# Feed-forward output products summed straight into the four quarters of the result, their operand differences by VectorE, and the recurrence's gate products grouped at its last chunk

## Chip, cores and metric

One core of a Trainium2 chip runs the whole kernel in one launch. The metric is the device time of that launch in microseconds, the median of the runs.

## What is computed

Two transformer blocks on one sequence of 1024 tokens and 1024 channels, all in float32. Each ends in a feed-forward part and only that and the second block's gated recurrence matter here:

```python
m = rmsnorm(h, g)
hid = square(relu(m @ w_in))       # 1024 -> 4096
h = h + hid @ w_out                # 4096 -> 1024, then the next norm

z = rms_norm(x, ln1_g) @ w_in + b_in               # second block
q, k, v, u, y_branch, g_att, g_rec = split(z)      # u, y, gates: 1024 channels each
u = centred_depthwise_conv(u, conv_w, conv_b)      # 4 taps
h_f, h_b = rg_lru(u, ..., reverse=False), rg_lru(u, ..., reverse=True)   # scans over tokens
y_rec = ((h_f + h_b) * gelu(y_branch)) @ w_rec_o
y_att = neighbourhood_attention(q, k, v, rpb) @ w_att_o
mixed = sigmoid(g_att) * y_att + sigmoid(g_rec) * y_rec
```

## The kernel before

Channels lie on partitions, tokens on the free axis: an activation of 1024 x 1024 is 8 tiles of 128 x 1024. Each float32 operand is split into a high and a low part, the high by ScalarE (`whi`, `obh`), the low by VectorE from it (`wlo`, `obl`, both line 478 for these blocks), and a product is three matmuls per 128 of its depth, high x high, high x low, low x high. The order of instructions on each engine is the program's own: `run` goes through a list of jobs, one product each, and before a job issues the weight splits that later jobs need (`ahead`, 3 jobs for the output products) and weight loads, all on SP's queue. 36 tiles of 128 x 1024 rotate for everything else (`z`).

**Feed-forward output.** The depth of 4096 goes in four blocks b = 0 to 3 (`N_BLK` is 3, the last one), each of 1024. In a block the 2 x 2 product of quarters is made of seven products of quarters (numbers 1, 2, 3, 6, 7, 5, 4, `SEVEN_OUT`) of sums and differences of the operands; each product is done for the four column pairs p of the result, 28 steps a block. A step is 12 matmuls of 512 columns into one of four PSUM banks (`seven`, line 1122); then deferred work (`todo`); at p = 0 and 2 the operand of the next product is prepared (`out_prep`: ScalarE and VectorE split it, and after four of the seven products GpSimd subtracts one quarter of the activation from another, lines 1200 to 1206, 128 x 1024 each); then the result is taken out of PSUM. In blocks 0 to 2 (`out_step`) that is one sum per step into one of seven partial sums `xs` (line 1274, VectorE; in block 0 ScalarE copies instead for products 1, 6, 7 and 5, line 1272). In block 2 the seven sums are mixed into the four quarters, by six GpSimd sums and two VectorE sums per p (line 1241). The residual `res` comes from HBM into `xs` before it is used (line 1238), in halves, mainly in block 0. The last block (`block_step` with `last_ev`) sums straight into the four quarters c11, c12, c21, c22 of `h`: eight VectorE sums, three GpSimd sums (lines 1327 to 1331) and one ScalarE copy per p. In the second feed-forward part the last block has an order of its own (`end_block`): product 2's operands are made beside product 1, its products are done late.

**The recurrence.** Channels go in 8 chunks c: a product for u, one for y, then gate products (`gate_job`), which only store their scaled result. 16 gate products are made: 6 before the chunks, 10 among them, one per chunk and two in chunks 3 and 7. Beside the products runs background work, generators in three lanes; `tick` after each six matmuls gives `rate` credits, and a whole credit takes one step of each lane. `lru_front` of a chunk (16 steps: convolution, the polynomial of gelu by GpSimd at lines 1741 and 1742, the gate matrices on TensorE at line 1766, their sigmoids by ScalarE at line 1753 behind the one of line 1759) starts when the chunk's y is there; `lru_back` (13 steps: ScalarE's functions, VectorE's scans, a store of the result at line 1801) follows it. The rate is 0.65, in chunk 7 1.0. `att2_split` prepares the attention's output operands during the last gate product. Then come eight attention output products (`att_o_job`, rate 1.1; `mixed` is written at line 1853 of it), which also load the recurrence's results, and the recurrence's output products.

Of the kernel before, what the change touches and what calls it, by code (L numbers as in the profile page):

```python
# [31 lines left out]
RATE_L = (0.65, 1.0)  # L32
# [164 lines left out]
class Kern:  # L197
# [992 lines left out]
    def out_prep(self, b, i, kk):  # L1190

        G = self.nc.gpsimd
        hi, lo = self.ob[b, i, kk] = self.u("obh"), self.u("obl")

        def q(e, a):
            return self.hraw[b, kk, e, a]

        self.hilo(q(0, 0) if i in (1, 7) else q(0, 1) if i == 5 else q(1, 0) if i in (2, 4) else q(1, 1), hi, lo)
        if i == 1:
            G.tensor_tensor(q(0, 1), q(0, 1), q(0, 0), ALU.subtract)  # L1200
        elif i == 3:
            G.tensor_tensor(q(1, 1), q(1, 1), q(0, 1), ALU.subtract)
        elif i == 6:
            G.tensor_tensor(q(0, 0), q(1, 1), q(0, 0), ALU.subtract)
        elif i == 7:
            G.tensor_tensor(q(1, 0), q(1, 0), q(1, 1), ALU.subtract)
            del self.hraw[b, kk, 0, 0], self.hraw[b, kk, 1, 1]
        elif i == 5:
            del self.hraw[b, kk, 0, 1]
        elif i == 4:  # L1210
            del self.hraw[b, kk, 1, 0]
# [6 lines left out]
    def out_step(self, un, b, p):  # L1218


        nc = self.nc
        V, G = nc.vector, nc.gpsimd
        i = un.i
        j = SEVEN_OUT.index(i)
        sl = slice((p % 2) * H, (p % 2) * H + H)

        def operand(k):
            ks = slice((k % 2) * H, (k % 2) * H + H)
            return tuple(x[:, ks] for x in self.ob[b, i, k // 2])

        def x(q):
            return self.xs[q, p // 2][:, sl]

        def alloc(q, e=None, a=None):
            if p % 2 == 0:
                self.xs[q, p // 2] = self.z(nm="xs")
            if e is not None:
                nc.sync.dma_start(x(q), half(self.res[2 * p + e], a))

        def add(eng, d, q):  # L1240
            eng.tensor_tensor(x(d), x(d), x(q), ALU.add)  # L1241

        def mix():
            if i == 2:
                add(G, 2, 1)
            elif i == 6:
                add(G, 6, 1)
                self.todo.append(lambda: self.todo.append(lambda: add(V, 3, 6)))
            elif i == 7:
                add(G, 7, 6)  # L1250
                alloc(0, 1, 1)
            elif i == 5:
                add(G, 3, 5)
                add(G, 5, 7)
            elif i == 4:
                add(G, 4, 7)
                add(V, 5, 0)
                self.h[2 * p], self.h[2 * p + 1] = [x(2), x(3)], [x(4), x(5)]

        def fn():  # L1260
            ps = self.seven(un, operand)
            todo, self.todo = self.todo, []
            for f in todo:
                f()
            for kk in AHEAD[p]:
                self.out_prep(*((b, SEVEN_OUT[j + 1]) if j < 6 else (b + 1, 1)), kk)
            self.next_loads(b + 1, i, p)
            if b == 0 and i in (1, 2, 5):
                alloc(*{1: (2, 0, 0), 2: (3, 0, 1), 5: (4, 1, 0)}[i])
            if b == 0 and i not in (2, 3, 4):  # L1270
                alloc(i)
                nc.scalar.activation(x(i), ps, AF.Copy)
            else:
                V.tensor_tensor(x(i), ps, x(i), ALU.add)  # L1274
            if b == N_BLK - 1:
                mix()
        return fn

    def block_step(self, un, b, p, ev, after, prep=True):
# [6 lines left out]
        def fn():  # L1286
            ps = self.seven(un, operand)
# [3 lines left out]
            if prep and i != SEVEN_OUT[-1]:  # L1291
                self.prep_step(b, i, p)()
            elif after:
                after(p)
# [16 lines left out]
    def last_ev(self, after):  # L1311
# [4 lines left out]
        def ev(i, p, ps):  # L1316
            u = self.half_u(i, p)
            (c11, c12), (c21, c22) = self.h[2 * p], self.h[2 * p + 1]
# [18 lines left out]
            after(i, p)  # L1337
        return ev

    def ff(self, pr, w1, w2, gname, after):  # L1340
# [44 lines left out]
        ev = self.last_ev(after)  # L1385
        n = 28
        for i in SEVEN_OUT:
            for p in range(4):
                un = two[i, p // 2]
                pr.job([un] if p % 2 == 0 else [], self.block_step(Pick(un, p % 2), N_BLK, p, ev, None),  # L1390
# [3 lines left out]
    def end_block(self, pr, two):  # L1394
# [3 lines left out]
        ev = self.last_ev(self.end_after)  # L1398
# [3 lines left out]
        for n, (i, p) in enumerate(order):  # L1402
# [5 lines left out]
            if i == 2:  # L1408
                pr.job(uns, self.prep_step(N_BLK, i, p), ahead)
                later.append(self.block_step(w, N_BLK, p, ev, None, False))  # L1410
# [4 lines left out]
            fn = self.end_step(w, p, (0, H // 2)) if i == 4 else self.block_step(w, N_BLK, p, ev, None)  # L1415
# [388 lines left out]
    def gate_job(self, un, dst, m, last=False):  # L1804
# [3 lines left out]
        def fn():  # L1808
            if last:
                self.bg[2].append(self.att2_split())  # L1810
# [3 lines left out]
            if last:  # L1814
# [66 lines left out]
    def program(self):  # L1881
        pr = Prog()
        self.h = [None] * NC
        self.hraw, self.ob, self.xs, self.todo = {}, {}, {}, []
# [136 lines left out]
        for c in range(NC):  # L2021
            pr.rate = RATE_L[c > NC - 2]
# [3 lines left out]
            gate_jobs(2 if c in (3, 7) else 1)  # L2026
# [223 lines left out]
```

## Time and profile before

| | |
|---|---|
| median of the runs | 2988.58 us (2981.69 to 2990.8, 3 runs) |
| the profiled execution | 2983.65 us, of which its span from the first to the last instruction 2981.9 us |
| busy share of the span | TensorE 96%, VectorE 64%, ScalarE 39%, GpSimd 37% |
| granted TensorE clock, mean | 0.985 |
| moved between HBM and the core | 402.35 MB |

First feed-forward output: 1074.5 to 1392 us of the span, blocks of about 76 us; second: 2637 to 2966. The recurrence's chunks: about 1736 to 2083, then the attention output products to 2136. PE is TensorE's matmuls, DVE VectorE, ACT ScalarE, POOL GpSimd, SP the engine that issues the DMAs. A row of a wait names who waited and who released it; a time in brackets in a row in order of time is how long the engine stood idle before it, and after the arrow who ended that. The share of the clock is that of TensorE's full speed.

### The profile page before, as it was taken

How to read it: one execution, taken by the hardware profiler on the slowest of the kernel's cores; microseconds unless marked ns; L12 is line 12 of the kernel's file. 1: busy time of each engine (PE TensorE's matmuls, PEld its weight loads, DVE VectorE, ACT ScalarE, POOL GpSimd, SP SyncE). 2: the span in 40 equal slices, each digit the busy share in tenths (PEclk: the TensorE clock that was granted, in tenths of full speed). 3: DMA queues.
4: the chain of work that ended last, by engine and by line, in shares of the span. 5: the costliest groups of instructions: out<-in, count | busy, mean ns of one | idle time of the engine just before them, and what ended most of it. 6: DMA issues, size and time to landing. Idle time of an engine off the chain costs nothing. (4 is left out here: it accounts for less than half of the span.)

```text
span 2981.9 us, 35224 instructions
## 1 busy us (share of the span) xinstructions
PE 2874.7 (96%) x13422; PEld 2357.2 (79%) x13422; DVE 1916.4 (64%) x2325; ACT 1170.6 (39%) x1786; POOL 1116.5 (37%) x554
## 2 busy tenths in 40 slices
PE   9999999999899999998999999998899899999987
PEld 8888787888788888876777788886788788888866
DVE  6434554666865577799743337878555855577797
ACT  3322234223354454335133325555423344444334
POOL 0020112644444443486300005455144444443486
PEclk9999999999999999999999999999999999999998
DMA  4221136776233254442423221221686233254442
GB/s 161 75 75 47 66 120 224 252 283 248 85 113 107 105 203 164 149 155 78 133 78 98 85 78 61 71 78 51 250 307 221 85 113 114 99 209 166 148 155 85
DMA packets 140056, 402.35 MB, mean 135 GB/s; under 512 B 14192, under 2 KB 32752, under 8 KB 139888
## 3 DMA queue, kind: packets, MB, share of 16 engines
q1 hardware_dynamic: 139888, 400.10, 38.5%
q8 instruction: 106, 1.74, 0.2%
q14 instruction: 62, 0.51, 0.1%
HBM read 287.75 MB, written 112.30 MB: 134 GB/s over the span
## 5 line engine op out<-in xcount | busy, mean ns | idle before, releaser
L1122 PE MATMUL bk<-obl,whi 128*128 128x512 f32 x864 | 339.3, 393 | 16.3 <-DVE obl L478 16.3
L477 ACT ACTIVATE whi<-raw 128x512 fp32r<-128x512 f32 (+2 forms) x256 | 205.1, 809 | 346.5 <-PE bk L1122 318.1
L1122 PE MATMUL bk<-obh,whi 128*128 128x512 f32 x864 | 338.0, 391 | 3.0 <-DVE xs L1334 2.0
L1122 PE MATMUL bk<-obh,wlo 128*128 128x512 f32 x864 | 338.1, 391 | 1.5 <-DVE wlo L478 1.5
L478 DVE TENSOR_TENSOR wlo<-raw,whi 128x512 fp32r<-128x512 f32 (+2 forms) x256 | 305.6, 1196 | 48.5 <-ACT whi L477 48.5
L439 PE MATMUL mm<-uh,whi 128*128 128x512 f32 x864 | 278.1, 403 | 6.7 <-DVE v L1554 5.2
L1122 PE MATMUL bk<-tt,whi 128*128 128x512 f32 x896 | 276.1, 389 | 0.2 <-DVE t L1158 0.2
L439 PE MATMUL mm<-ul,whi 128*128 128x512 f32 x864 | 269.6, 393 | 2.2 <-DVE ul L491 2.2
L378 POOL TENSOR_TENSOR wsum<-wsum 128x1024 f32<-128x1024 f32 x64 | 181.6, 2848 | 237.6 <-DMA wsum<-in_w 235.0
L439 PE MATMUL mm<-uh,wlo 128*128 128x512 f32 x864 | 267.8, 391 | 0.0
L339 DVE TENSOR_TENSOR wlo<-raw,whi 128x1024 fp32r<-128x1024 f32 (+3 forms) x140 | 221.6, 1589 | 33.9 <-ACT whi L338 33.8
L478 DVE TENSOR_TENSOR obl<-hraw,obh 128x1024 fp32r<-128x1024 f32 x112 | 196.9, 1758 | 28.5 <-ACT obh L477 25.4
L439 PEld LDWEIGHTS mm<-uh,whi 128*128 128x128 f32 x864 | 157.2, 190 | 64.7 <-issue 32.9
L1122 PEld LDWEIGHTS bk<-obl,whi 128*128 128x128 f32 x864 | 163.1, 189 | 55.1 <-DVE obl L478 21.3
L1122 PEld LDWEIGHTS bk<-tt,whi 128*128 128x128 f32 x896 | 168.1, 188 | 35.6 <-issue 0.6
L439 PEld LDWEIGHTS mm<-ul,whi 128*128 128x128 f32 x864 | 163.4, 189 | 39.0 <-DVE ul L491 4.0
L1122 PEld LDWEIGHTS bk<-obh,whi 128*128 128x128 f32 x864 | 163.1, 189 | 37.9 <-DVE xs L1334 2.4
L1122 PEld LDWEIGHTS bk<-obh,wlo 128*128 128x128 f32 x864 | 163.2, 189 | 36.2 <-DVE wlo L478 2.7
L439 PEld LDWEIGHTS mm<-uh,wlo 128*128 128x128 f32 x864 | 162.9, 189 | 35.4 <-DVE wlo L339 0.5
L338 ACT ACTIVATE whi<-raw 128x1024 fp32r<-128x1024 f32 (+3 forms) x140 | 135.6, 975 | 132.6 <-PE mm L670 63.8
L1122 PE MATMUL bk<-tt,wlo 128*128 128x512 f32 x448 | 174.3, 389 | 0.0
L1741 POOL TENSOR_SCALAR yt<-yt 128x1024 f32<-128x1024 f32 x8 | 16.8, 2100 | 411.8 <-DMA sgr<-sgr 302.7
(364 smaller groups left out, 6421.4 us busy)
## 6 DMA issues: line engine op xcount, KB each, us to landing
raw<-in_w SPq DMA_DIRECT2D x190, 512.0 KB
wsum<-in_w SPq DMA_DIRECT2D x64, 512.0 KB
sums<-wsum SPq DMA_DIRECT2D x64, 512.0 KB
hraw<-hid SPq DMA_DIRECT2D x64, 512.0 KB
raw<-sums SPq DMA_DIRECT2D x64, 512.0 KB
hid<-h SPq DMA_DIRECT2D x56, 512.0 KB
wraw<-in_w SPq DMA_DIRECT2D x28, 512.0 KB
rb<-in_rpb SPq DMA_DIRECT2D x24, 384.0 KB
```

The costliest lines, as they stand in the source:

```text
L338: nc.scalar.activation(un.hi, un.raw, AF.Copy)
L339: nc.vector.tensor_tensor(un.lo, un.raw, f32(un.hi), ALU.subtract)
L378: G.tensor_tensor(d, x, y, f)
L439: nc.tensor.matmul(dst[a], w, half(x, a), start=(i == 0 and q == 0), stop=(i == n - 1 and q == 2),)
L477: self.nc.scalar.activation(hi, src, AF.Copy)
L478: self.nc.vector.tensor_tensor(lo, src, f32(hi), ALU.subtract)
L1122: nc.tensor.matmul(ps, w[:, k * P:(k + 1) * P], x, start=(k == 0 and q == 0), stop=(k == n - 1 and q == 2))
L1741: G.tensor_scalar(t, t, 0.044715, 1.0, ALU.mult, ALU.add)
```

## The change

The partial sums `xs` and the mixing go: every block uses `block_step` and the evacuation of the last block (`last_ev`, now `out_ev`). The residual is loaded into `h`, whole tiles, two per step, ahead of the four steps of product 1 in block 0. The four subtractions of `out_prep` go from GpSimd to VectorE, in all blocks. In the recurrence the rate is 0.7 throughout; the ten gate products among the chunks are 0, 1, 1, 1, 1, 1, 1, 4 per chunk instead of 1, 1, 1, 2, 1, 1, 1, 2, and `att2_split` starts one gate product earlier.

```diff
@@ -29,7 +29,7 @@
-RATE_L = (0.65, 1.0)
+RATE_L = 0.7
@@ -1189,7 +1189,7 @@
 
-        G = self.nc.gpsimd
+        V = self.nc.vector
         hi, lo = self.ob[b, i, kk] = self.u("obh"), self.u("obl")
@@ -1197,13 +1197,13 @@
         if i == 1:
-            G.tensor_tensor(q(0, 1), q(0, 1), q(0, 0), ALU.subtract)
+            V.tensor_tensor(q(0, 1), q(0, 1), q(0, 0), ALU.subtract)
         elif i == 3:
-            G.tensor_tensor(q(1, 1), q(1, 1), q(0, 1), ALU.subtract)
+            V.tensor_tensor(q(1, 1), q(1, 1), q(0, 1), ALU.subtract)
         elif i == 6:
-            G.tensor_tensor(q(0, 0), q(1, 1), q(0, 0), ALU.subtract)
+            V.tensor_tensor(q(0, 0), q(1, 1), q(0, 0), ALU.subtract)
         elif i == 7:
-            G.tensor_tensor(q(1, 0), q(1, 0), q(1, 1), ALU.subtract)
+            V.tensor_tensor(q(1, 0), q(1, 0), q(1, 1), ALU.subtract)
             del self.hraw[b, kk, 0, 0], self.hraw[b, kk, 1, 1]
@@ -1215,68 +1215,8 @@
-    def out_step(self, un, b, p):
...
-        def alloc(q, e=None, a=None):
-            if p % 2 == 0:
-                self.xs[q, p // 2] = self.z(nm="xs")
-            if e is not None:
-                nc.sync.dma_start(x(q), half(self.res[2 * p + e], a))
-
-        def add(eng, d, q):
-            eng.tensor_tensor(x(d), x(d), x(q), ALU.add)
-
-        def mix():
-            if i == 2:
-                add(G, 2, 1)
-            elif i == 6:
-                add(G, 6, 1)
-                self.todo.append(lambda: self.todo.append(lambda: add(V, 3, 6)))
-            elif i == 7:
-                add(G, 7, 6)
-                alloc(0, 1, 1)
-            elif i == 5:
-                add(G, 3, 5)
-                add(G, 5, 7)
-            elif i == 4:
-                add(G, 4, 7)
-                add(V, 5, 0)
-                self.h[2 * p], self.h[2 * p + 1] = [x(2), x(3)], [x(4), x(5)]
-
-        def fn():
-            ps = self.seven(un, operand)
-            todo, self.todo = self.todo, []
-            for f in todo:
-                f()
-            for kk in AHEAD[p]:
-                self.out_prep(*((b, SEVEN_OUT[j + 1]) if j < 6 else (b + 1, 1)), kk)
-            self.next_loads(b + 1, i, p)
-            if b == 0 and i in (1, 2, 5):
-                alloc(*{1: (2, 0, 0), 2: (3, 0, 1), 5: (4, 1, 0)}[i])
-            if b == 0 and i not in (2, 3, 4):
-                alloc(i)
-                nc.scalar.activation(x(i), ps, AF.Copy)
-            else:
-                V.tensor_tensor(x(i), ps, x(i), ALU.add)
-            if b == N_BLK - 1:
-                mix()
-        return fn
...
-    def block_step(self, un, b, p, ev, after, prep=True):
+    def block_step(self, un, b, p, ev, prep=True):
+
         i = un.i
@@ -1284,14 +1224,20 @@
         def fn():
+            if (b, i) == (0, 1):
+                for m in (2 * p, 2 * p + 1):
+                    self.h_load(m, self.res)
             ps = self.seven(un, operand)
                 self.prep_step(b, i, p)()
-            elif after:
-                after(p)
+            elif b < N_BLK:
+                for kk in AHEAD[p]:
+                    self.out_prep(b + 1, 1, kk)
+            if b < N_BLK:
+                self.next_loads(b + 1, i, p)
             ev(i, p, ps)
@@ -1308,14 +1254,14 @@
 
-    def last_ev(self, after):
+    def out_ev(self, after=None):
 
             u = self.half_u(i, p)
-            (c11, c12), (c21, c22) = self.h[2 * p], self.h[2 * p + 1]
+            c11, c12, c21, c22 = (half(self.h[2 * p + e], a) for e in range(2) for a in range(2))
             if i == 1:
@@ -1334,7 +1280,8 @@
                 V.tensor_tensor(c21, ps, c21, ALU.add)
-            after(i, p)
+            if after:
+                after(i, p)
         return ev
@@ -1373,7 +1320,7 @@
                     un = two[i, p // 2]
-                    steps.append(((un, None)[p % 2], self.out_step(Pick(un, p % 2), b, p)))
+                    steps.append(((un, None)[p % 2], self.block_step(Pick(un, p % 2), b, p, self.out_ev())))
         end = after == self.end_after
@@ -1801,17 +1748,17 @@
 
-    def gate_job(self, un, dst, m, last=False):
+    def gate_job(self, un, dst, m, left):
 
         def fn():
-            if last:
+            if left == 1:
                 self.bg[2].append(self.att2_split())
             nc.sync.dma_start(dst[m], t)
-            if last:
+            if left == 0:
                 self.us = [None] * NC
@@ -2014,16 +1961,16 @@
                 pr.job([un := Unit("w_in_2", 0, NC, col + P * m, P)],
-                       self.gate_job(un, dst, m, not gates), ahead)
+                       self.gate_job(un, dst, m, len(gates)), ahead)
         gate_jobs(5)
         for c in range(NC):
-            pr.rate = RATE_L[c > NC - 2]
+            pr.rate = RATE_L
             uu = Unit("w_in_2", 0, NC, 1536 + P * c, P)
             self.uy_jobs(pr, uu, uy, c)
-            gate_jobs(2 if c in (3, 7) else 1)
+            gate_jobs((0, 1, 1, 1, 1, 1, 1, 4)[c])
         pr.rate = 1.1
```

## Rows read from the trace of the kernel before

**Rows 1.** The page: busy us, share, instructions; group obl: busy, mean ns, idle before.

```profile
PE 2874.7 (96%) x13422; PEld 2357.2 (79%) x13422; DVE 1916.4 (64%) x2325; ACT 1170.6 (39%) x1786; POOL 1116.5 (37%) x554
...
L478 DVE TENSOR_TENSOR obl<-hraw,obh 128x1024 fp32r<-128x1024 f32 x112 | 196.9, 1758 | 28.5 <-ACT obh L477 25.4
```

**Rows 2.** Table by stretch, the recurrence: us, busy (x instructions) by engine, clock, DMA.

```profile
1983.00:2018.00 35.00, 35.00 (x156) 29.01 (x155) 31.05 (x18) 19.31 (x22) 17.65 (x6) 1.00 0.12 38
2018.00:2083.00 65.00, 52.35 (x207) 41.35 (x206) 56.45 (x37) 33.62 (x40) 35.12 (x12) 0.89 0.17 57
2083.00:2136.00 53.00, 47.22 (x198) 37.67 (x196) 35.27 (x31) 32.59 (x34) 7.64 (x3) 0.97 0.62 233
```

**Rows 3.** The same table, output blocks of the first and second feed-forward part.

```profile
1151.00:1227.00 76.00, 76.00 (x337) 62.94 (x336) 60.46 (x56) 28.18 (x28) 23.56 (x8) 1.00 0.46 152
1227.00:1304.00 77.00, 75.36 (x331) 61.74 (x331) 69.05 (x59) 28.43 (x28) 55.26 (x25) 1.00 0.48 158
1304.00:1370.00 66.00, 62.52 (x273) 50.50 (x272) 64.62 (x51) 23.47 (x25) 54.59 (x24) 1.00 0.30 96
...
2789.00:2865.00 76.00, 74.36 (x327) 60.90 (x327) 67.85 (x57) 28.41 (x28) 53.65 (x23) 1.00 0.50 167
2865.00:2949.00 84.00, 74.70 (x312) 60.39 (x311) 75.01 (x64) 36.87 (x47) 68.15 (x33) 0.94 0.19 63
```

**Rows 4.** TensorE's waits, 2018 to 2142: waiter, releaser, us, times, longest.

```profile
PE bk L1766 <- ACT gt L1753: 10.9, 2, 6.6
PE mm L439 <- DVE mixed L1853: 5.7, 3, 3.2
PE mm L439 <- DVE wlo L339: 3.9, 1, 3.9
```

**Rows 5.** Order of time around chunk 6's gates: start, us, instruction, [idle, releaser].

```profile
2009.95 0.63 ACT L477 ACTIVATE rgh<-rgr 128x512 fp32r<-128x512 f32 x1 [7.98 <-DMA rgr<-in_rg]
...
2020.47 0.75 DVE L1738 TENSOR_SCALAR y<-y,cst 128x1024 f32<-128x1024 f32 x1
...
2025.61 3.18 POOL L1742 TENSOR_TENSOR yt<-yt,y 128x1024 f32<-128x1024 f32 x1
...
2028.82 1.06 ACT L1759 ACTIVATE yt<-yt 128x1024 f32<-128x1024 f32 x1 [5.20 <-POOL yt L1742]
```

**Rows 6.** Order of time, chunk 3's third gate group on TensorE.

```profile
1903.63 0.19 PEld L1766 LDWEIGHTS bk<-uch,rgh 128*128 128x128 f32 x1 [0.26 <-ACT gt L1753]
```

**Rows 7.** TensorE's waits, 2789 to 2949.

```profile
PE bk L1122 <- DVE obl L478: 10.9, 5, 4.7
```

**Rows 8.** Order of time at the end of block 2, second part.

```profile
2870.61 3.32 POOL L1200 TENSOR_TENSOR hraw<-hraw 128x1024 f32<-128x1024 f32 x1
2871.65 3.35 DVE L478 TENSOR_TENSOR obl<-hraw,obh 128x1024 fp32r<-128x1024 f32 x1
...
2875.06 0.80 PE L1122 MATMUL bk<-obl,whi 128*128 128x512 f32 x1 [4.73 <-DVE obl L478]
```

**Rows 9.** Lines by instruction: ns least/median/most, first and last start, form.

```profile
L478 DVE TENSOR_TENSOR obl<-hraw,obh x29: 1207/1219/3366, 1075.4 to 1222.9; 128x1024 fp32r<-128x1024 f32 x29
...
L523 DVE TENSOR_TENSOR sq<-sq x16: 1214/1225/3411, 23.1 to 2319.2; 128x1024 f32<-128x1024 f32 x16
...
L1274 DVE TENSOR_TENSOR xs<-bk,xs x136: 676/686/693, 1089.0 to 2878.8; 128x512 f32<-128x512 f32 x136
...
L1330 POOL TENSOR_TENSOR xs<-xs,uu x8: 1288/1298/2289, 1360.9 to 2932.9; 128x512 f32<-128x512 f32 x8
```

**Rows 10.** Start of block 0, first part: a stretch; SP and VectorE in time.

```profile
1065.00:1079.00 14.00, 13.85 (x61) 11.16 (x60) 8.98 (x9) 6.99 (x10) 6.07 (x3) 1.00 1.04 406
...
1076.79 0.33 SPq L1175 DMA_DIRECT2D hid<-h  x1
1079.90 0.33 SPq L1149 DMA_DIRECT2D hid<-h  x1
...
1083.72 1.23 DVE L478 TENSOR_TENSOR obl<-hraw,obh 128x1024 fp32r<-128x1024 f32 x1 [0.21 <-ACT obh L477]
```

More of the change, by code (lines that the diff above doesn't have):

```diff
@@ L1216, in next_loads @@
             self.out_load(b, p % 2, e, (p // 2) ^ e)
-    def out_step(self, un, b, p):
[L1221 to L1232, printed above, removed]
-        def alloc(q, e=None, a=None):
-            if p % 2 == 0:
-                self.xs[q, p // 2] = self.z(nm="xs")
-            if e is not None:
-                nc.sync.dma_start(x(q), half(self.res[2 * p + e], a))
-        def add(eng, d, q):
-            eng.tensor_tensor(x(d), x(d), x(q), ALU.add)
-        def mix():
-            if i == 2:
-                add(G, 2, 1)
-            elif i == 6:
-                add(G, 6, 1)
-                self.todo.append(lambda: self.todo.append(lambda: add(V, 3, 6)))
-            elif i == 7:
-                add(G, 7, 6)
-                alloc(0, 1, 1)
-            elif i == 5:
-                add(G, 3, 5)
-                add(G, 5, 7)
-            elif i == 4:
-                add(G, 4, 7)
-                add(V, 5, 0)
-                self.h[2 * p], self.h[2 * p + 1] = [x(2), x(3)], [x(4), x(5)]
-        def fn():
-            ps = self.seven(un, operand)
-            todo, self.todo = self.todo, []
-            for f in todo:
-                f()
-            for kk in AHEAD[p]:
-                self.out_prep(*((b, SEVEN_OUT[j + 1]) if j < 6 else (b + 1, 1)), kk)
-            self.next_loads(b + 1, i, p)
-            if b == 0 and i in (1, 2, 5):
-                alloc(*{1: (2, 0, 0), 2: (3, 0, 1), 5: (4, 1, 0)}[i])
-            if b == 0 and i not in (2, 3, 4):
-                alloc(i)
-                nc.scalar.activation(x(i), ps, AF.Copy)
-            else:
-                V.tensor_tensor(x(i), ps, x(i), ALU.add)
-            if b == N_BLK - 1:
-                mix()
-        return fn
-    def block_step(self, un, b, p, ev, after, prep=True):
+    def block_step(self, un, b, p, ev, prep=True):
         i = un.i
@@ L1384, in ff @@
             return
-        ev = self.last_ev(after)
+        ev = self.out_ev(after)
         n = 28
@@ L1389, in ff @@
                 un = two[i, p // 2]
-                pr.job([un] if p % 2 == 0 else [], self.block_step(Pick(un, p % 2), N_BLK, p, ev, None),
+                pr.job([un] if p % 2 == 0 else [], self.block_step(Pick(un, p % 2), N_BLK, p, ev),
                        3 if n >= 3 else 2)
@@ L1397, in end_block @@
         self.acc, self.sqs = {}, {}
-        ev = self.last_ev(self.end_after)
+        ev = self.out_ev(self.end_after)
         later = []
@@ L1409, in end_block @@
                 pr.job(uns, self.prep_step(N_BLK, i, p), ahead)
-                later.append(self.block_step(w, N_BLK, p, ev, None, False))
+                later.append(self.block_step(w, N_BLK, p, ev, False))
                 continue
@@ L1414, in end_block @@
                     pr.job([], fn, ahead)
-            fn = self.end_step(w, p, (0, H // 2)) if i == 4 else self.block_step(w, N_BLK, p, ev, None)
+            fn = self.end_step(w, p, (0, H // 2)) if i == 4 else self.block_step(w, N_BLK, p, ev)
             pr.job(uns, fn, ahead)
@@ L1883, in program @@
         self.h = [None] * NC
-        self.hraw, self.ob, self.xs, self.todo = {}, {}, {}, []
+        self.hraw, self.ob, self.todo = {}, {}, []
         self.uu = {}
```

## Prediction

> **What bounds the kernel now.** I read the busy times of the page first: TensorE is busy for 2874.7 of the 2981.9 us of the span [rows 1], so a change can only win what TensorE waits. Next, tables by stretch, and in them one quotient: TensorE's busy time over its matmuls in a stretch where it never waits, as a price per matmul; the matmuls of the next stretch at that price against its length give what is lost there, the waits and the lower clock after them together. Before the recurrence's end 156 matmuls take 35.00 us, 0.2244 us each; then 207 take 65.00 (46.4 are needed, 18.6 lost) and 198 take 53.00 (8.6 lost) [rows 2]; the granted clock, 1.00 before, falls to a mean of 0.89 in the first of these, so each long wait costs more than itself. In the first feed-forward part block 1 is the clean one: 337 matmuls in 76.00 us, 0.2255 each. The stretch that is mostly block 2 loses 77.00 - 331 x 0.2255 = 2.4 us, most of block 3 66.00 - 273 x 0.2255 = 4.4; in the second part it is 2.3 and 84.00 - 312 x 0.2255 = 13.6 [rows 3]. All stretches that the change touches hold 27.2 + 6.8 + 15.9 = 49.9 us: more can't be won.
>
> Third, the waits and the order of time there. In the recurrence TensorE waited 10.9 us for ScalarE's gate sigmoids and 5.7 for VectorE's `mixed` [rows 4]. In the output blocks it waited for the low parts `obl`, 10.9 us between 2789 and 2949 [rows 7], and the rows show why: GpSimd's subtraction took 3.32 us, VectorE's split 3.35 beside it, and TensorE stood for 4.73 [rows 8]. An operation of either engine with two SBUF inputs waits for the other's: VectorE's split takes 1.22 us as a rule and 3.37 at most, GpSimd's 512-wide sum 1.29 or 2.29 [rows 9]. VectorE's sum of a product, one input from PSUM, takes 0.68 to 0.69 always [rows 9].
>
> **The recurrence.** The last chunk now has rate 0.7 instead of 1.0, and four gate products instead of two. A step of the background work comes after each 1/rate of a matmul group (six matmuls, 1.35 us): 1.35 us apart before, 1.92 after. In chunk 6 the bias of y is added at 2020.47, GpSimd ends the polynomial at 2028.8, the sigmoid starts at 2028.82, and the gate sigmoids that release PSUM stand behind it on ScalarE [rows 5]; TensorE's third gate group was there 6.6 us too early [rows 4]. Between the step that adds y and that group lie 7 steps: 0.57 us more each, 4.0 us in all (of 6.6), and chunk 6 is no longer crowded by its late weights, since its load also stood behind a store (7.98 us of wait for rgr) [rows 5]: that store is now issued about 4 steps before the load instead of 2. Chunk 7's front needs 16 steps; it gets 32 groups x 0.7 = 22, so 7 steps of its back part, with the ScalarE functions, also run beside gates and not beside the attention output products, where they made `mixed` late. What speaks against a full win: chunks 0 to 6 go from 0.65 to 0.7, 0.14 x 7 = 1.0 us less cover each, and chunk 3 at 0.65 was already just late (0.26 us) [rows 6]. I leave 3.5 us for two or three chunks, and the 0.6 us of a wait for `wlo` that begins in the last stretch and is an order of VectorE's that isn't touched [rows 4]. Gain 27.2 - 0.6 - 3.5 = 23 us; bounds 12 (half) and 27. Moving chunk 0's gate away costs no TensorE time: there are as many products. The gate stores on SP move with the products, each still directly behind its own evacuation, so no load is put behind an older wait.
>
> **The output blocks, steady state.** Removed per feed-forward part: 24 GpSimd and 8 VectorE sums of block 2, 16 copies by ScalarE, and 16 half-tile loads. Added in each of blocks 0 to 2: the eight VectorE sums of each of 4 column pairs (32; before, 12 in block 0 and 28 in blocks 1 and 2), 12 GpSimd sums and 4 ScalarE copies, as block 3 has now; moved in all four blocks: 8 subtractions of 128x1024 from GpSimd to VectorE. VectorE has not done this subtraction; the nearest row is its 128x1024 sum of squares, 1.23 us [rows 9] (bounds 1.21 and, beside GpSimd, 3.4). VectorE's work in a block: 28 splits and 8 subtractions x 1.22 + 32 sums x 0.69 = 66.0 us; TensorE's: 336 x 0.2255 = 75.8 us. Between lies what GpSimd's 12 sums hold up: nothing to 12 x 1.29 = 15.5 us. Block 1 of the trace prices it: 28 x 1.22 + 28 x 0.69 = 53.5 us of work took 60.46, so 7.0 lost beside 23.56 us of GpSimd [rows 3, 9], 0.30 us per us. With 12 sums of at most 2.29 us: 8 us, so 74 of 75.8 us. Followed product by product: products 2, 3 and 6 carry two subtractions (9.9 us of 10.8), 7 carries GpSimd's eight sums, 5 double sums (10.4); I find VectorE at most 2.3 us behind, after product 5, and level again by the next product 1. A split for the second half of an operand has some 4 us of room, so no wait. The mix of block 2 goes, and with it the backlog on both engines that the waits of blocks 2 and 3 came from. Of the 6.8 us I keep 1.0; of the 15.9 us 3.5, since the last block of the second part still does two products' splits at once. Gain 5.8 + 12.4 = 18.2 us. Its cover is those 1.8 us a block; without it see the last rival. At the end of the first part h is now whole tiles, so one operation of the next norm runs where two halves ran: the same elements, I cost it at nothing, within 1 us either way, the wait of the halves for each other.
>
> **The start of block 0.** New: eight whole tiles of h are loaded inside product 1, two per step, and the first sums wait for them; before, block 0's sums of product 1 were ScalarE copies that waited for no load. The queue is full then: 406 GB/s, 1.04 of the engines [rows 10], so 512 KB take 1.29 us. On SP the first two stand behind the store of 1076.79, h0 lands near 1081; the next behind the store of 1079.90 [rows 10], which itself moves some 1.2 us with the subtraction on VectorE, and a weight piece: h2 lands near 1087 to 1088. The sum of (1, 1) waits for it, and queued behind that on VectorE is the low part for the second half of product 2, done at 1084.95 now [rows 10], then at 1088.9 to 1090. TensorE wants it at 1074.8 + 10.8 + 1.4 = 1087: a stall of 1.9 to 3, and the lower clock behind it. The trace shows no such wait; bounds are nothing (the loads in time) and 8 us (h6 lands near 1094, 9 us after TensorE's product, less a little room). I take 3.5 per part, 7 in all.
> The Trainium skill ("DMA: Bandwidth & Descriptors", Rules for kernel authors) says to issue a DMA early and wait for its semaphore late; the load here is issued in the step that uses it. By that rule the whole order of eight loads would be paid, the 8 us above; by the rows most of it is hidden behind ScalarE's own delay.
>
> **Sum.** 23 + 18.2 - 7 = 34 us. The profiled execution took 2983.65 us, the median of the runs is 2988.58, 4.9 above it; waits don't depend on that, so 2983.65 - 34 = 2950 for it and 2988.6 - 34 = 2954.6 for the median. I forecast 2955.
>
> **Rivals.**
> A. The loads of h cost their upper bound, 8 us and as much as 3 of lower clock in each part: 2955 + 15 = 2970. For it: the full queue [rows 10]. Against: the first sums are already late for another reason.
> B. The even pace of 0.7 is itself too fast with chunk 3 as the model: a wait of about 1.5 us, with its clock, in every chunk, 12 instead of 3.5, and the `mixed` waits stay: 2955 + 14 = 2969. For it [rows 6]; against it that other chunks show no wait at 0.65 [rows 2].
> C. The waits only move: VectorE needs 80 us a block, 4.2 over TensorE's, 8 blocks, 34 us: 2955 + 34 = 2989, no change.
> D. Slower: VectorE bounds all output blocks. Place: the 36 operations with two SBUF inputs of each block; each GpSimd sum holds one up for its whole time (66.0 + 15.5 = 81.5), and VectorE waits 3 us more per block for ScalarE's high parts, as it does now (25.4 us in 8 blocks [rows 1]). 84.5 - 75.8 = 8.7 us x 8 = 70 us against the 41 won: 2989 - 41 + 70 + 7 = 3025. It decides from 81 us of VectorE per block upward. Against it: 0.30 us per us above.
> The Trainium skill ("SBUF — State Buffer", SBUF: two separate sides) has the port that VectorE and GpSimd share as an exclusive lock, in which the loser waits for the whole instruction. Rows 8 and 9 agree (3.35 against 1.22 us); were every GpSimd sum to win the lock, that is D's price.
>
> **Chances.** Forecast 0.56 (2942 to 2966), A 0.15, B 0.14, C 0.09, D 0.06. A measurement of this kernel tells about 0.3%, 9 us, from no change. Faster by more: forecast, A, B, 0.85; within: 0.09; slower: 0.06. The range leaves C and D out, takes A and B in, and below the forecast the bound of all 49.9 us less little: 2938 to 2981.
>
> **What would show it.** Right: no wait over 1 us for `gt` near 2020 to 2080; the stretch from 1983 to the recurrence's output products shorter by 23; no GpSimd operation on `hraw`; VectorE at about 74 of 76 us in blocks 0 to 2 without waits for `obl` there; one or two waits for `obl` of 1 to 3 us at product 2 of block 0. Wrong: waits for `obl` through all blocks (D, C), a long wait for a load of h on VectorE (A), waits for `gt` in chunks 1 to 5 (B).

## The result, and the profile after

The changed kernel takes 2951.22 us (median of 4 runs, 2947.18 to 2952.86) beside 2987.72 us for the kernel before: a ratio of 0.9878, 95% interval 0.986 to 0.9897, so 36.5 us faster. The forecast was 2955 us. The profiled execution is the slowest of the four (2952.86 us; its span 2951.0), that of before one of the faster: the two traces stand only 30.9 us apart, and sizes by place are read from the traces, the total from the medians.

The page after: busy us, share and instructions, and the group of the low parts `obl` [rows 1].

```profile
PE 2866.5 (97%) x13422; PEld 2355.2 (80%) x13422; DVE 1915.4 (65%) x2421; ACT 1160.3 (39%) x1754; POOL 975.8 (33%) x506
...
L478 DVE TENSOR_TENSOR obl<-hraw,obh 128x1024 fp32r<-128x1024 f32 x112 | 155.3, 1387 | 13.9 <-ACT obh L477 10.8
```

VectorE does 96 instructions more in the same time: a low part takes 1387 ns in the mean instead of 1758, since fewer GpSimd instructions run beside it.

The table by stretch for the recurrence [rows 2], columns as there. It ends some 20 us earlier than before; the last stretch reaches to the wait for `wlo`.

```profile
1880.00:1910.00 30.00, 27.29 (x113) 21.75 (x111) 26.59 (x14) 20.04 (x23) 16.39 (x6) 0.94 0.16 53
1910.00:2000.00 90.00, 88.85 (x391) 73.03 (x390) 84.93 (x59) 50.13 (x55) 47.30 (x16) 1.00 0.23 81
2000.00:2083.00 83.00, 83.00 (x367) 68.64 (x367) 76.02 (x48) 49.74 (x56) 43.99 (x14) 1.00 0.30 106
2083.00:2116.00 33.00, 33.00 (x147) 27.29 (x146) 19.32 (x20) 19.13 (x20) 0.00 (x0) 1.00 0.72 278
```

By the prediction's quotient (0.2244 us per matmul) the first loses 30.00 - 113 x 0.2244 = 4.6 us, the second 2.3, the third 0.6, the last nothing. Where 27.2 us were lost there is no wait left. TensorE's waits from 1880 to 2125 (waiter, releaser, us, times, longest) [rows 4]:

```profile
PE mm L439 <- DVE wlo L339: 3.9, 1, 3.9
PE bk L1713 <- ACT gt L1700: 2.7, 1, 2.7
PE mm L439 <- DVE zu L472: 1.1, 1, 1.1
```

(From the recurrence on, lines are 53 lower: L1713 is L1766 of before, L1700 L1753, L1685 L1738.) The waits for `mixed` are gone, `wlo` is as before, and one wait for `gt` stands in chunk 3, in the first stretch.

The output blocks of both parts [rows 3]:

```profile
1160.00:1236.00 76.00, 76.00 (x337) 62.90 (x337) 66.26 (x69) 30.19 (x32) 23.79 (x12) 1.00 0.44 151
1236.00:1312.00 76.00, 76.00 (x337) 62.94 (x336) 66.25 (x69) 30.20 (x32) 23.79 (x12) 1.00 0.45 152
1312.00:1370.00 58.00, 58.00 (x258) 48.02 (x257) 49.12 (x50) 23.22 (x25) 21.06 (x11) 1.00 0.29 94
...
2788.00:2864.00 76.00, 76.00 (x337) 62.94 (x336) 70.17 (x72) 32.88 (x36) 23.79 (x12) 1.00 0.51 166
2864.00:2920.00 56.00, 56.00 (x251) 46.20 (x250) 46.77 (x51) 29.68 (x38) 30.44 (x18) 1.00 0.18 57
```

TensorE is busy in every microsecond of them; in blocks 1 and 2 of the first part VectorE needs 66.3 of 76 us, not 74.

The start of block 0 in the first part [rows 10], SP, VectorE and TensorE in order of time (start, us, instruction, in brackets the idle time and its releaser):

```profile
1078.57 1.15 SPq L1007 DMA_DIRECT2D h<-res  x2
1082.66 0.32 SPq L1149 DMA_DIRECT2D hid<-h  x1
...
1083.54 3.48 SPq L1007 DMA_DIRECT2D h<-res  x4
...
1090.69 0.69 DVE L1268 TENSOR_TENSOR h<-bk,h 128x512 f32<-128x512 f32 x1 [4.12 <-DMA h<-res]
1091.30 1.22 DVE L478 TENSOR_TENSOR obl<-hraw,obh 128x1024 fp32r<-128x1024 f32 x1
...
1092.57 0.50 PE L1122 MATMUL bk<-obl,whi 128*128 128x512 f32 x1 [3.17 <-DVE obl L478]
...
1093.88 0.63 PE L1122 MATMUL bk<-obh,whi 128*128 128x512 f32 x1
```

Four whole tiles of h are issued behind the store of 1082.66. VectorE's second sum waits 4.12 us for one of them, the low part of product 2 stands behind that sum, TensorE waits 3.17 us for the low part, and from 1093.88 on seven of its matmuls are 0.63 us long instead of 0.39. The second part has the same: 3.1 us at 2630, and thirteen slow matmuls.

### The profile page after: what moved, and what is told of

It is laid out like the page before. It is cut to its first block, busy times and chain, and to the rows that moved or that the text cites. A ratio compares the mean times of both kernels' runs of the same rounds, so it can differ in the third digit from the quotient of the medians.

```text
span 2951.0 us, 35195 instructions
## 1 busy us (share of the span) xinstructions
PE 2866.5 (97%) x13422; PEld 2355.2 (80%) x13422; DVE 1915.4 (65%) x2421; ACT 1160.3 (39%) x1754; POOL 975.8 (33%) x506
## 5 line engine op out<-in xcount | busy, mean ns | idle before, releaser
L478 DVE TENSOR_TENSOR wlo<-raw,whi 128x512 fp32r<-128x512 f32 (+2 forms) x256 | 255.4, 1001 | 39.0 <-ACT whi L477 39.0
L1273 POOL TENSOR_TENSOR h<-h,uu 128x512 f32<-128x512 f32 x32 | 70.9, 2227 | 382.6 <-DVE uu L1272 382.6
L1122 PEld LDWEIGHTS bk<-tt,whi 128*128 128x128 f32 x896 | 168.0, 188 | 36.5 <-issue 1.6
L1122 PEld LDWEIGHTS bk<-obh,whi 128*128 128x128 f32 x864 | 163.2, 189 | 36.5 <-DVE h L1280 2.0
L478 DVE TENSOR_TENSOR obl<-hraw,obh 128x1024 fp32r<-128x1024 f32 x112 | 155.3, 1387 | 13.9 <-ACT obh L477 10.8
```

The source lines that it names most:

```text
L478: self.nc.vector.tensor_tensor(lo, src, f32(hi), ALU.subtract)
L1122: nc.tensor.matmul(ps, w[:, k * P:(k + 1) * P], x, start=(k == 0 and q == 0), stop=(k == n - 1 and q == 2))
L1273: G.tensor_tensor(c12, c12, u, ALU.add)
```

## Experiments

Each kernel was timed in 4 or 5 runs against the kernel before on the same chip, whose median there was 2985 to 2986 us. The changed kernel itself stands at 0.9878, and a ratio's interval is about 0.0013 to 0.0019 either way, 4 to 6 us, so differences between two kernels below some 5 us are read from the traces, not from the times. "Lost" below is a sum over TensorE's 512-column matmuls: the time from one start to the next beyond 0.227 us.

**e1, the recurrence's part alone**, on the kernel before:

```diff
-RATE_L = (0.65, 1.0)
+RATE_L = 0.7
...
-            gate_jobs(2 if c in (3, 7) else 1)
+            gate_jobs((0, 1, 1, 1, 1, 1, 1, 4)[c])
```

> The kernel before with the recurrence part of the change alone (pace 0.7 throughout, gate products 0, 1, 1, 1, 1, 1, 1, 4, the attention operands one gate product earlier). Theory (each part wins in its own place, nothing is handed on): the trace after lost 12.3 us to waits and the lower clock between 1800 and 2200 where the trace before lost 32.7, so 20 us of the 36.5 are from here: 2988 - 20 = 2968, and the wait near 1892 of the trace after (2.7 us, released by a gate sigmoid of chunk 3) is here too, since it is of this part. Rival (the parts share: the feed-forward work that follows moves with the recurrence): 2960 or 2978.

2965.5 us, ratio 0.9932 (0.992 to 0.9945): 20.0 us gained. The waits are those of the kernel after, 2.5 us for `gt` in chunk 3 among them.

**e2, the output blocks' part alone**: the kernel after with those lines, and the start of `att2_split`, as before.

> The kernel after with the recurrence as it was before: the output blocks' part alone. Theory: in the first feed-forward output the losses fell by 3, in the second by 10.6, so 2988 - 14 = 2974, with the waits for gt near 2020 to 2080 and for mixed back in their old size (10.9 and 5.7 us). Rival (the parts are not independent): 2966 or 2982.

2970.7 us, ratio 0.9951 (0.9938 to 0.9965): 14.9 us gained, the waits for `gt` and `mixed` back at 12.1 and 5.5 us. 20.0 + 14.9 = 34.9 of 36.5: the two parts add up.

**e3, the differences back on GpSimd**, in the kernel after:

```diff
-        V = self.nc.vector
+        G = self.nc.gpsimd
...
-            V.tensor_tensor(q(0, 1), q(0, 1), q(0, 0), ALU.subtract)
+            G.tensor_tensor(q(0, 1), q(0, 1), q(0, 0), ALU.subtract)
```

(and the other three alike)

> The kernel after with the eight differences of activations per block back on GpSimd; the straight sums stay. Theory (the wait for a low part came from a difference on GpSimd that holds VectorE's split beside it and delays the next product's operand, 3.3 us each): waits for obl come back in every block, GpSimd at 24 + 8 x 2.3 to 3.3 = 42 to 50 of 76 us, VectorE's work 8 x 1.22 less but 0.3 x 20 = 6 us of holding more; half of what the second part lost before, so 6 to 10 us over the kernel after: 2957 to 2961. Rival (the mixing of block 2 alone made the waits, the engine of the differences is of no matter): within 2 us of the kernel after, 2951.

2961.3 us, ratio 0.9921 (0.9908 to 0.9933), 24.2 us under the kernel before: 12 us less than the change brings by the times, 8.5 by the spans. Waits for `obl` come back, but not in every block as expected; three new ones are over 1 us, 1.7 and 1.6 us in product 6 of block 0 of the two parts and 1.9 us in the last block of the second. Block 1 has none:

```profile
1161.00:1237.00 76.00, 76.00 (x337) 62.94 (x336) 69.56 (x62) 30.21 (x32) 48.90 (x20) 1.00 0.46 154
```

VectorE is busier than in the kernel after (66.26), though it has eight differences fewer to make.

**e11, the differences on VectorE alone**, in the kernel before: the same edit the other way round; partial sums and mixing stay.

> The kernel before with the eight differences per block on VectorE and all else as it was, the partial sums and their mixing in block 2 too. Theory (two causes: the differences on GpSimd, worth 8.5 us in the trace of the kernel after with them back, and the mixing): 8 to 12 us off the kernel before, 2974 to 2978 against 2986; waits for obl in block 2 and 3 of the second part that are left are behind the mixing's sums. Rival (the mixing alone makes the waits): 2983 to 2986. Second rival (the differences alone do, the straight sums bring nothing and cost the start of block 0): 2986 minus the whole 16 to 19 lost there, 2967 to 2970, less than the output part of the change reached (2970.7).

2975.5 us, ratio 0.9967 (0.9954 to 0.9979): 9.6 us gained. TensorE's waits from 2789 to 2949 fall from 10.9 [rows 7] to 7.1 us, those that the mixing of block 2 leaves (splits beside GpSimd's mixing sums take 2.28 to 2.32 us there). The stretch that answers the first of [rows 3], and the waits:

```profile
1151.00:1227.00 76.00, 76.00 (x337) 62.94 (x336) 59.60 (x65) 28.15 (x28) 0.00 (x0) 1.00 0.45 152
```

```profile
PE bk L1122 <- DVE obl L478: 7.1, 2, 5.1
```

This is the price of the move: VectorE was busy for 60.46 us while GpSimd subtracted, and is busy for 59.60 when it subtracts itself. The eight differences cost it nothing. The straight sums, once the start of block 0 is paid, bring the rest, some 4 to 5 us, if the parts add up (14.9 - 9.6 by e2 and e11, 24.2 - 20.0 by e3 and e1; no more than an interval).

**e10, GpSimd's sums to VectorE too**, in the kernel after:

```diff
-                G.tensor_tensor(c12, c12, u, ALU.add)
+                V.tensor_tensor(c12, c12, u, ALU.add)
```

(and c22 and c21)

> The kernel after with the twelve half-tile sums per block that GpSimd makes made by VectorE too, so GpSimd has nothing in the output blocks. VectorE was busy for 66.3 of 76 us in block 1 of the trace after; twelve sums of 128x512 with two SBUF inputs are 0.68 each, 8.2 us, and the holding by GpSimd goes. Theory (GpSimd held VectorE for some 0.2 to 0.3 us per us of its own 23.8, 5 to 7 us): VectorE at 67 to 70 of 76 us; product 7 alone has 15 us of VectorE's work against TensorE's 10.8, so low parts come 1 to 3 us late behind it in every block: 8 blocks, 8 to 24 us more, 2959 to 2975. Rival one (only the sum over a block counts): within 4 us of 2951. Rival two (each GpSimd sum holds VectorE for its whole time, some 24 us per block): VectorE below 55 us and no slower, 2951.

2950.7 us, ratio 0.989 (0.9876 to 0.9903): no change. My theory fell, rival one stands: blocks 1 and 2 show no wait. I had counted 15 us of VectorE's work for product 7; from its first sum to the first one of product 5 it is 12.3 us, against TensorE's 10.9. In the last block of the second part TensorE does wait 1.9 us for a VectorE sum, which it doesn't in the kernel after. The stretch of block 1, and the first sums of products 7 and 5:

```profile
1160.00:1236.00 76.00, 76.00 (x337) 62.94 (x336) 69.27 (x80) 30.04 (x33) 0.00 (x0) 1.00 0.46 153
...
1203.18 0.68 DVE L1275 TENSOR_TENSOR uu<-bk,uu 128x512 f32<-128x512 f32 x1
...
1215.44 0.69 DVE L1279 TENSOR_TENSOR h<-bk,h 128x512 f32<-128x512 f32 x1
```

**e4, the residual's loads spread**, in the kernel after:

```diff
+                4: [(self.h_load, (0, self.res))],
-                3: [(self.out_prep, (0, 1, 1))]}
+                3: [(self.out_prep, (0, 1, 1)), (self.h_load, (2, self.res))]}
...
-            if (b, i) == (0, 1):
-                for m in (2 * p, 2 * p + 1):
-                    self.h_load(m, self.res)
+            if b == 0 and (i, p) in ((1, 0), (1, 1)):
+                self.h_load(2 * p + 4, self.res)
+            if (b, i) == (0, 2):
+                self.h_load(2 * p + 1, self.res)
```

> The kernel after with the loads of the residual spread: h0 and h2 two products of the input half earlier, h4 and h6 in the first two steps of product 1, the odd tiles, which product 7 needs first, in product 2. Theory (the stall at product 2 of block 0 and the lower clock behind it come from the order of eight whole tiles on a full queue): the stalls of 3.2 us at 1089 and 3.1 at 2630 with their low clock, 4.8 + 5.9 us, shrink to under 1 us each: 2951 - 9 = 2942. Rival (product 1's sums on VectorE are late for VectorE's own work, the loads are only the last of several): the waits of VectorE for h go, the stalls stay over 2 us, 2949 to 2951. Second rival: the earlier loads delay the loads of weights and hidden activations that stand behind them on the queue, and a new stall of 1 to 3 us comes before block 0.

2941.5 us, ratio 0.9851 (0.9838 to 0.9865), as forecast. Both stalls are gone with their clock; the stretches around them, first of the kernel after, then of this one:

```profile
1070.00:1100.00 30.00, 26.84 (x112) 21.51 (x111) 17.97 (x20) 15.42 (x20) 1.29 (x1) 0.94 0.97 372
2610.00:2650.00 40.00, 36.53 (x148) 29.25 (x147) 27.76 (x31) 18.88 (x24) 1.29 (x1) 0.91 0.80 306
```

```profile
1070.00:1100.00 30.00, 30.00 (x133) 24.60 (x132) 23.44 (x26) 17.09 (x23) 1.28 (x1) 1.00 0.99 385
2610.00:2650.00 40.00, 40.00 (x177) 32.83 (x176) 33.91 (x38) 22.32 (x27) 1.29 (x1) 1.00 0.79 305
```

The DMA engines are as full as in the kernel after (0.99 and 0.97): not the amount but the order and the moment on SP made the stall. h0 and h2 now go out together, ahead of both stores; in the kernel after, h2 went out behind the second one, at 1083.54:

```profile
1073.80 1.57 SPq L1007 DMA_DIRECT2D h<-res  x2
1079.48 0.32 SPq L1175 DMA_DIRECT2D hid<-h  x1
```

The edit also issues the odd tiles later; which of the two did more was not separated.

**e5, the pace at 0.65**, in the kernel after:

```diff
-RATE_L = 0.7
+RATE_L = 0.65
```

> The kernel after with 0.65 in place of 0.7 as the pace of all eight chunks, the gate products as in the change. Theory (what was won in the last chunk came from no longer running at 1.0, and 0.65 gives each step 0.14 us more cover): no wait for gt near the last two chunks, the wait of chunk 3 (2.7 us at 1892) shorter by the 7 steps x 0.14 = 1.0 us and its clock less: 2948 to 2951. Rival (a chunk's front part needs 16 steps and gets 24 matmul groups x 0.65 = 15.6, so it falls behind by 0.4 steps a chunk, and the last chunk's back part ends beside the attention output products): waits for mixed come back, 3 to 6 us, 2954 to 2957.

2943.2 us, ratio 0.986 (0.9846 to 0.9873): better than theory and rival. Between 1800 and 2000 nothing is lost (6.5 us in the kernel after), and a wait for `mixed` of 1.3 us is back: 4.1 us less lost from 1800 to 2200. The rest lies at the starts of block 0, which the edit doesn't touch: they lose 7.7 us in this trace, 12.2 in that of the kernel after. Why chunk 3 is freed is seen on VectorE, first in the kernel after, then at 0.65:

```profile
1882.34 1.22 DVE L472 TENSOR_TENSOR sgr<-mm,rstd 128x1024 f32<-128x1024 f32 x1
1885.46 1.23 DVE L339 TENSOR_TENSOR wlo<-raw,whi 128x1024 fp32r<-128x1024 f32 x1 [1.91 <-ACT whi L338]
1886.60 0.74 DVE L1685 TENSOR_SCALAR y<-y,cst 128x1024 f32<-128x1024 f32 x1
```

```profile
1873.36 1.22 DVE L472 TENSOR_TENSOR sgr<-mm,rstd 128x1024 f32<-128x1024 f32 x1
1874.49 1.22 DVE L339 TENSOR_TENSOR wlo<-raw,whi 128x1024 fp32r<-128x1024 f32 x1
...
1880.97 0.74 DVE L1685 TENSOR_SCALAR y<-y,cst 128x1024 f32<-128x1024 f32 x1
```

At 0.7 the step that adds y's bias falls just behind the end of a gate product: on VectorE it stands behind that product's evacuation and a weight split that waits for ScalarE. At 0.65 the product's end falls some steps earlier, and y waits for nobody.

**e12, y's step first**, in the kernel after: the steps "bias, square, polynomial of y" and "split of uc" exchanged.

> The kernel after, with two steps of each chunk's background work exchanged: y's bias, square and polynomial come one step before the split of the convolution's result instead of behind it. In chunk 3 of the trace after, y's bias (1886.6) stood on VectorE behind the evacuation of a gate product and a weight split that waited 1.9 us for ScalarE, and GpSimd's polynomial and the gate sigmoids came late by as much. Theory (chunk 3's wait is the place of y's step against the end of a product): y's bias comes before that evacuation, 5 us earlier, the wait of 2.7 us near 1892 and its lower clock go, 3 to 5 us off: 2946 to 2948, as at the pace of 0.65, where y's bias stood before the evacuation. Rival (the pace of 0.7 is too short for the steps behind y, wherever y falls): the wait stays over 1 us, 2949 to 2951. Second rival: the split of the convolution's result, now a step later, falls behind the same evacuation, and TensorE's first gate group waits for it, 1 to 3 us: 2950 to 2953.

2947.8 us, ratio 0.9871 (0.9855 to 0.9888): not to be told from the kernel after. The wait for `gt` in chunk 3 goes, and one for the split of `uc`, which now stands behind the same evacuation and weight split, takes its place, as the second rival has it. Between 1800 and 2000 5.1 us are lost, little less than the 6.5 of the kernel after:

```profile
PE bk L1713 <- ACT uch L477: 2.2, 1, 2.2
PE bk L1713 <- DVE ucl L478: 0.5, 1, 0.5
```

**e8, the residual's loads spread and the gate matrices loaded earlier**, with the chunk's u product:

```diff
+            self.rgr = self.ph.tile([P, 512], F32, tag="rgr", name="rgr", bufs=1)
+            nc.sync.dma_start(self.rgr, self.ins["rg"][c])
...
-        raw = self.ph.tile([P, 512], F32, tag="rgr", name="rgr", bufs=1)
-        nc.sync.dma_start(raw, self.ins["rg"][c])
+        raw = self.rgr
```

In this kernel chunk 0 is computed with the gate matrices of chunk 1; kind and amount of the work are the same.

> The kernel with the residual's loads spread (2941.5 us) and the recurrence's gate matrices loaded one product earlier, beside the chunk's u product instead of at the start of its background work. Theory (chunk 3's wait is that of a load put behind a store that waited 4 us for VectorE: matrices late, then VectorE's order late, then GpSimd's polynomial and the gate sigmoids): the wait near 1892, 2.7 us, and its lower clock go, 3 to 4.5 us: 2937 to 2938.5. Rival (at 0.7 the step order itself is too short in chunk 3, the load only adds to it): 2940 to 2941.5, a wait of 1 to 2 us stays there.

2939.2 us, ratio 0.9846 (0.9832 to 0.9859), not to be told from e4. Chunk 3's load is issued at 1836.43, in the kernel after at 1871.62, and chunk 3's wait stays:

```profile
1836.43 0.66 SPq L1656 DMA_DIRECT2D rgr<-in_rg  x1
...
PE bk L1717 <- ACT gt L1704: 2.3, 1, 2.3
```

So a late load, to which the prediction gave a share of chunk 6's trouble, isn't what makes the wait of chunk 3; e12 shows what does. For chunk 6 of the kernel before it was not tested.

**e6, the pace at 0.7 with the old gate products, and e7, the new gate products with 1.0 in the last chunk**, in the kernel after:

```diff
-            gate_jobs((0, 1, 1, 1, 1, 1, 1, 4)[c])
+            gate_jobs(2 if c in (3, 7) else 1)
```

```diff
-            pr.rate = RATE_L
+            pr.rate = (RATE_L, 1.0)[c > NC - 2]
```

> The kernel after with the gate products 1, 1, 1, 2, 1, 1, 1, 2 per chunk again, at the pace of 0.7. Theory (two causes: the pace removes the waits for gt, 10.9 us; the four products of the last chunk remove those for mixed, 5.7 us, since its back part, seven steps and more, has the room): no gt wait near the last two chunks, waits for mixed and a lower clock back, 6 to 9 us: 2957 to 2960; the wait of chunk 3 goes, since its store falls elsewhere, -3: 2954 to 2957. Rival (the pace alone does it): 2948 to 2951.

> The kernel after with pace 1.0 in the last chunk again, and its four gate products. Theory: the waits for gt come back, 6.6 and 4.3 us with a lower clock behind each, those for mixed don't: 11 to 14 us over the kernel after, 2962 to 2965. Rival (the number of gate products did it, the pace is of no matter): 2951.

2967.8 us (0.9945, 0.9932 to 0.9957) and 2967.4 us (0.9946, 0.9933 to 0.996): each 18 to 19 us under the kernel before, little more than the output part gains alone (14.9). Between 2000 and 2200 the kernel before lost 32.2 us, e6 32.0, e7 25.0, the kernel after 5.8. Neither half of the edit brings much by itself. TensorE's waits there, e6 first:

```profile
PE mm L439 <- DVE mixed L1800: 11.8, 4, 6.1
PE mm L439 <- DVE sgr L472: 5.5, 1, 5.5
```

```profile
PE mm L439 <- DVE mixed L1800: 5.8, 1, 5.8
...
PE bk L1713 <- ACT gt L1700: 3.4, 1, 3.4
```

In e6 the waits for `gt` are nearly gone (0.7 us) and those for `mixed` doubled: the last chunk's back part now runs wholly beside the attention output products. (The 5.5 us for `sgr` are for the last gate product's evacuation, which stands behind the scan and two products of chunk 6's back part on VectorE.) ScalarE there has its functions ahead of the gate `gin` that `mixed` needs:

```profile
2087.26 2.19 ACT L1729 ACTIVATE gt<-gt,cneg 128x1024 f32<-128x1024 f32 x2
...
2090.77 2.00 ACT L1732 ACTIVATE th<-th 128x1024 f32<-128x1024 f32 x2
2092.79 1.28 ACT L944 ACT_TABLE_LOAD   x1
2094.08 1.15 ACT L944 ACTIVATE gin<-gin,cst 128x1024 f32<-128x1024 f32 x1
```

In e7 the waits for `gt` come back only in part (3.4 us), and, against the theory, one for `mixed` as well. The functions were done in time, and `mixed` is late by another way, which I had not foreseen: VectorE's scans hold up the recurrence's last result and the evacuation of the last gate product, so their stores and the load of `gin` behind them on SP come late, and ScalarE waits for that load:

```profile
2093.11 1.28 ACT L944 ACT_TABLE_LOAD   x1 [9.90 <-DMA gin<-sg]
```

**e9, combined**: e4, e5, and in `program`

```diff
-            pr.job([un], self.att_o_job(un, m), 2 if m < NC - 1 else None)
+            pr.job([un], self.att_o_job(un, m), 2)
```

> The residual's loads spread (2941.5 us), the pace at 0.65 with the change's gate products (2943.2), and the weights of the first of the recurrence's output products split before the last attention output product instead of behind it (the split stands behind the operands of the recurrence on VectorE, TensorE waited 3.9 us near 2107 to 2116 in all kernels so far). Theory (three waits in three places, independent): 2951.2 - 9.8 - 4.0 (the recurrence's 5 us less the 1 us that the last chunk gives back) - 5.9 (wait and lower clock) = 2931.5. Rival (the split, once early, stands in front of an order that the attention output products wait for, or the next weights are late): the wait near 2107 moves on, 2936.

2931.0 us, ratio 0.9817 (0.9804 to 0.9831): 54 us under the kernel before, about 18 better than the change. Between 1740 and 2140 one wait is left; the wait for `wlo` is gone and didn't move:

```profile
PE mm L439 <- DVE mixed L1803: 1.1, 1, 1.1
```

## Why the prediction was right, step by step

| step | predicted | trace after against before | alone |
|---|---|---|---|
| recurrence, 1800 to 2200 | -23 | 32.7 to 12.3 lost: -20.4 | e1: -20.0 |
| output blocks behind their start (1200 to 1500, from 2800 on) | -18.2 | 24.4 to 16.5 and 16.7 to 0.2 lost: -24.4 | |
| start of block 0 (1000 to 1100, 2600 to 2700) | +7 | 0.4 to 5.2 and 1.1 to 7.0 lost: +10.7 | e4: -8 by the ratios |
| output blocks in all | -11.2 | -13.7 | e2: -14.9 |
| sum | -34 | -34.1 | -36.5 by the medians |

The sum came out right while two terms of opposite sign were off by 6.2 and 3.7 us and the first by 2.6: that it came so close is in part luck, since these errors cancel. (The spans of the two traces differ by 30.9 us, not 34.1; some 3 us are lost in stages that the change doesn't touch.)

**Recurrence: right in place, and partly in reason.** The waits for `gt` in chunks 6 and 7 and for `mixed` went. "I leave 3.5 us for two or three chunks" was one chunk, 3, and a `zu` wait behind it, 6.5 us with the clock. The step that failed in it is the reckoning of chunk 3's wait in cover per step (0.14 x 7): e5 and e12 show that it is a matter of which step of the background falls behind the end of a product, and e8 that the late load of the matrices, on which I leaned for chunk 6, is not needed for such a wait. That pace and gate products are one cause and not two was in the sentence on the 22 steps of chunk 7, but the price of either alone was not seen: e6 and e7 came 11 to 14 and 2 to 5 us above what I expected of them.

**Output blocks, steady state: right in direction, mis-sized.** The term was VectorE's time per block: 66.0 us of work and 8 of holding, 74. Measured: 66.3. Both parts were too large. The 66.0 added up durations; but VectorE's 1.22 us instructions start 1.14 us apart (1885.46 and 1886.60 above), so their sum counts overlaps twice. And GpSimd's sums hold less than the price taken from block 1 of before: e10, without them, has VectorE busy for 69.3 us with twelve sums more, about 0.6 us of start to start each, so 62 of its own in the kernel after, and 4 held, not 8. The 0.30 us per us came from a block in which GpSimd only subtracted, and I carried it over to its sums. For the subtractions e11 gives more: 8 x 1.14 = 9.1 us of work were added and the busy time fell by 0.9, so 10 us had been held by 23.56 of GpSimd, 0.42 per us. For the 512-wide sums it is 4 / 23.8 = 0.17. (e3 has both: 69.6 - (62 - 9.1) = 16.7 us held by 48.9.)

With 10 us of room per block instead of 1.8 no wait was left in blocks 1 and 2 (the 3.5 kept in the second part were 0.2), and e10 could put 8 us more on VectorE there without one. The product by product reckoning ("at most 2.3 us behind", so no wait) stands: even in e10, where product 7 takes VectorE 1.4 us more than TensorE, no wait follows in these blocks. (Products with two subtractions come to 6 x 1.22 + 4 x 0.69 = 10.1 us, not 9.9, and product 4 carries two as well.) At the first part's tail the whole tiles cost "nothing, within 1 us", as written: TensorE waits 2.6 us for ScalarE's half of the next norm's split and 0.3 for VectorE's, where it waited 0.2 and 2.2.

The Trainium skill ("SBUF — State Buffer", SBUF: two separate sides) has the loser of the shared port wait for the whole instruction. The trace after agrees case by case: in block 1 seven of VectorE's instructions with two SBUF inputs took over 1.3 us, and each ended 1.08 to 1.09 us behind the end of a GpSimd sum, about the 1.14 us that one needs from start to start: it did its work when the sum had ended. Here the sum ends at 1220.41 and the low part at 1221.50:

```profile
1219.10 1.31 POOL L1277 TENSOR_TENSOR h<-h,uu 128x512 f32<-128x512 f32 x1
1219.25 2.25 DVE L478 TENSOR_TENSOR obl<-hraw,obh 128x1024 fp32r<-128x1024 f32 x1
```

But not every GpSimd instruction meets one of VectorE's, and then only its rest is waited for: the mean was 0.17 to 0.42 us per us, and rival D, which took 1, is out.

**Start of block 0: right mechanism, and nearly the size.** The chain (store, queue, h2, the sum of (1, 1), the low part of product 2, TensorE) came as written. I had h2 land at 1087 to 1088 and the low part done by 1090; they were 1090.7 and 1092.5, since the store ahead of the loads went out at 1082.66, not 1081, and four tiles and a weight piece followed at once. The stall was 3.2 us where 1.9 to 3 stood, and the clock behind it 7 x 0.20 = 1.4 and 13 x 0.20 = 2.6 us (slow matmuls start 0.43 us apart, others 0.23). That makes 10.7 us against 7, but in the slowest execution: in e2, e5, e6, e7 and e12, whose output blocks are the same code, the two starts lose 7.7 to 9.9 us, 6.2 to 8.4 more than in the kernel before. Rival A (8 us a part and clock) stays wrong; e4 shows that the whole price was avoidable. By the Trainium skill ("DMA: Bandwidth & Descriptors", Rules for kernel authors) a DMA is issued early and waited for late; the trace of e4 agrees: with h2 issued 9.7 us earlier TensorE waits there no more.

**Rivals.** B has its wait in one chunk, not in each; C and D fall with the 66.3 us.

## What to carry to other kernels

Before an instruction is moved from GpSimd to VectorE to spare a latency, weigh what it holds up where it is: here eight differences of 128x1024 cost VectorE as much while GpSimd made them as when it made them itself. Background work that is stepped by TensorE's progress can be late by its phase, even where its mean pace suffices: look which step falls behind a product's evacuation, and change the pace or its place against the product, and then look which step stands there now (in e12 another took its place). When sums go straight into a residual, its loads become part of the first products' chain, so issue them before the stores that wait for compute and in the order of use.

## What was not expected of the hardware

VectorE's busy time fell under the sum of its durations (66.3 against 70.3 us in one block), as consecutive instructions overlap by 0.08 us; capacity is better added from start to start. And a GpSimd sum of 128x512 is itself held: 1.29 us at its shortest, 2.2 to 2.29 for nine of the twelve in block 1, four of them here:

```profile
L1276 POOL TENSOR_TENSOR h<-h,uu x4: 2271/2274/2289, 1205.4 to 1216.9; 128x512 f32<-128x512 f32 x4
```

(ns least, median, most.) After the wait of 3.2 us in the first part seven matmuls ran at half clock (1.2 of 2.4 GHz), after that of 3.1 in the second thirteen. In e6 a wait of 3.2 us at the first of these places was followed by none, and the granted clock stayed at 1.00:

```profile
PE bk L1122 <- DVE obl L478: 3.2, 1, 3.2
...
1080.00:1100.00 20.00, 16.83 (x74) 13.59 (x73) 10.20 (x12) 11.53 (x15) 0.82 (x1) 1.00 0.89 345
```

So waits of nearly one length cost in clock from nothing to 2.6 us; what decides it is not shown here. Much of the spread of the starts of block 0 between runs of the same code comes from it.
